# Three small reorderings in a one-core decoder layer: a low half behind a sum, two block loads dealt anew, and a stage's first loads one tile sooner

## The chip, the cores and the metric

The kernel runs on one core of a Trainium2 chip. The metric is the time of one execution on the device in microseconds (us), as the median of several runs. A profiled execution gives, besides its own time, a span: from the first to the last instruction on the core.

The engines are named as in the profile: PE is TensorE doing matmuls, PEld its weight loads (which overlap with the matmuls), DVE is VectorE, ACT is ScalarE, POOL is GpSimd, and SP (SPq) is the queue from which nearly all DMAs are issued. DMAs move data between the chip's main memory and the on-chip tiles; PSUM banks are where matmuls add up their results.

## The reference

One layer of a decoder over 1040 tokens (16 meta tokens and 1024 inputs), width 1024, float32. Cut to what matters here:

```python
a = rmsnorm(h, ln_mix_pre)
proj = a @ w_in                                    # 1024 x 3584
y_diff = diff_attention(...)                       # four heads, 512 wide
y_hgrn = hgrn2(...)                                # four heads, 512 wide
mix = concatenate([y_diff, y_hgrn], -1) @ w_out    # 1024 x 1024
h = h + rmsnorm(mix, ln_mix_post)
a = rmsnorm(h, ln_ffn_pre)
u = conv3(a @ w_up) + conv_b                       # 1024 x 5632, causal depthwise, width 3
gate, up = split(u, 2)
y = (gelu(gate) * up) @ w_down                     # 2816 x 1024
h = h + rmsnorm(y, ln_ffn_post)
return h[16:]                                      # meta tokens dropped
```

## The kernel before

**Precision.** Every float32 operand of a matmul is split into a high half (a cast to `fp32r` on ACT) and a low half (operand minus high half, on DVE or POOL): `split`, line 148. A product is then three matmuls: high by high, high by low, low by high. In the profile the halves of weights are `wh` and `wl` (`uh` and `ul` in the up stage), those of the down stage's left operand `gh` and `gl`, and those of the up stage's activations are both `t`.

**Order of the work.** PE runs in exactly the order of the program text. For every other engine and for the DMA queue a planner decides the order, from its own estimate of times and with the earlier text first where several things are ready; each engine then works its list strictly in that order. `tc.issue_after(x)` puts what is issued inside it behind `x` in the planned order. A tile (buffer) with a tag is reused by the next tile of that tag, and whoever writes it next waits until its last reader is done. So a change in the text moves both the planner's lists and the waits.

**Out-projection, second half of the columns** (loop at line 1281). Nine blocks of tokens, block 0 the meta tokens. For block `i` of 1 to 8, PE multiplies the block's mixed rows (1 MB with both halves, loaded from `msc` in two pieces by `second_load`, lines 1048 and 1055) with the weights `wo`. Three buffers hold blocks: "X1", "X2" and "mp". `SLOTS[1]` (line 1039) says which block uses which. At iteration `i` block `i + 1` is loaded and then the residual rows `xh` of block `i + 1` (`load_xh`, line 1190, two buffers). `post(i)` (line 1198) normalizes and adds the residual on ACT and DVE, stores the sum to `hsc`, and makes the normed rows `a2` (`a` in the profile); `trans(i - 2)` transposes an earlier block's normed rows on PE (line 1237) and ACT copies them to `at2` (`at`). After blocks 5 and 7 `t_split` splits finished quarters of `at2` for the up stage; the quarters 7 and 6 go into the buffers X2 and X1 that blocks have left.

**Up stage** (loop at line 1492, with `unit`, line 1372). The hidden width of 2816 is cut into 22 tiles `ft`; each tile has gate and up columns. The two halves of the contraction, of the tokens and gate against up make a 2 by 2 by 2 product that is done with seven products instead of eight (sums of weight quarters and of activation quarters are formed ahead). Tile 0 is done plainly. For the others, `unit(ft, p)` is one tile for token half `p`; both halves step in turn through products 0 to 6, each twelve matmuls (lines 1383 to 1385), into three PSUM banks: products 0 and 4 into `pa`, 1, 3 and 5 into `pb`, 2 and 6 into `pc`. Between them the partial results are read: ACT copies `x1` from `pa` after product 0, DVE forms u2 = pb + x1 after product 1, u3 = pb + x1 after product 3, and the outputs `uu` and `ug`. In the profile u2 and u3 are both `u`. Product 3 adds into the bank that u2 reads, so it must wait for u2, and likewise product 5 for u3. `gated` (line 1346) does the convolution (`c`), the gelu and the product, and stores to `gsc`. While tile `ft` is multiplied, `prep(7 * (ft + 1) + j)` (line 1139) prepares weight `j` of the next tile, at the head of step `j`: a sum of quarters on POOL (`w_sum`, for j of 0, 1, 3 and 6), the cast on ACT, the low half on POOL for j of 2, 4 and 6 and on DVE for j of 0, 1, 3 and 5.

**Down stage** (from line 1608). Seven products again, each over 11 pairs of tiles; `operands` loads and splits one pair, `LOOK` = 3 pairs ahead of PE (`ahead`, line 1530); the matmuls are at lines 1543 to 1545 (`pd`). The first three pairs are loaded (`opens`) and split inside the last tile of the up stage, at lines 1501 to 1506; with four buffers for `gi` and five for `wi`, the latter shared with the raw up weights.

Of the kernel before, what the change touches and what calls it, by code (L numbers as in the profile page):

```python
# [24 lines left out]
NF = DFF // P  # L25
HEADS = 4
NBLK = 9
# [58 lines left out]
def layer_kernel(ctx: ExitStack, tc: tile.TileContext, x, meta, table, lbl, gpre, gpost, win,  # L86
# [3 lines left out]
    V, A = Ordered(tc, nc.vector, state), Ordered(tc, nc.scalar, state)  # L90
    G = Ordered(tc, nc.gpsimd, state)
# [56 lines left out]
    def split(hi, lo, raw, eng=None, after=None):  # L148
        A.copy(hi, raw)
        with nullcontext() if after is None else tc.issue_after(after.ins):  # L150
            low = (eng or G).tensor_tensor(lo, raw, hi.bitcast(F32), op=ALU.subtract)
        if eng in (None, G):
            lows.append(low)
# [645 lines left out]
    raws, parts = {}, [[None, None] for _ in range(3)]  # L799
# [236 lines left out]
                yield from out_part(m0_7, py, wo[KD - 1:], range(1), False, False)  # L1036


    SLOTS = (("X1", "X2", "mp", "X1", "X2", "mp", "X1", "X2"), ("mp", "X1", "X2", "mp", "X1", "X2", "X1", "mp"))

    def block_tile(n, i):
        tag = SLOTS[n][i - 1]
# [12 lines left out]
    def second_load(i):  # L1055
        blocks[i] = block_tile(1, i)
        block_load(blocks[i], i, 0, 4)
        block_load(blocks[i], i, 4, 7 if i == 1 else 8)
# [63 lines left out]
    at2.reverse()  # L1122
    q_cm, qp = pool("p2", 2, "right")

    raws, sums, made = {}, {}, {}

    def load_raw4(ft):
        raws.clear()
# [10 lines left out]
    def prep(q):  # L1139
        ft, j = divmod(q, 7)  # L1140
        if ft >= NF or q in made:
            return
        if j == 0:
            load_raw4(ft)
            src = raws["11"]
            w_sum("1", raws["21"], raws["22"], ALU.add)
        elif j == 1:
            src = w_sum("2", sums["1"], raws["11"], ALU.subtract)
        elif j == 2:
            src = sums["1"]  # L1150
        elif j == 3:
            src = w_sum("3", raws["11"], raws["21"], ALU.subtract)
        elif j == 4:
            src = raws["12"]
        elif j == 5:
            src = raws["22"]
        else:
            src = w_sum("4", raws["12"], sums["2"], ALU.subtract)
        where = swp if q % 2 else wp
        hi = where.tile([P, 512], F32R, tag="wh", name=f"uh{q}", bufs=4)  # L1160
        lo = where.tile([P, 512], F32R, tag="wl", name=f"ul{q}", bufs=4)
        split(hi, lo, src, G if j % 2 == 0 and j else V)
        made[q] = (hi, lo)

    plain = {}
# [87 lines left out]
    def t_split(p, j, src, where, *tag):  # L1253
        hi, lo = t_tiles(p, j, where, tag)
        A.copy(hi, src)
        V.tensor_tensor(lo, src, hi.bitcast(F32), op=ALU.subtract)
        tt[p][j] = (hi, lo)

    def quarter(p, j):
        n = WN[p]  # L1260
        a, c = {0: (0, 0), 7: (0, n), 4: (4, 0), 6: (4, n)}[j]
        return at2[p][:, a:a + 4, c:c + n]
# [18 lines left out]
    for i in range(1, NBLK):  # L1281
        py = ps_b(f"py1_{i}")
        if i >= 3:
            y0_gain(i)
        if i == 1:
            load_xh(1)
            load_xh(0)
        if i + 1 < NBLK:
            second_load(i + 1)
            load_xh(i + 1)  # L1290
        run(blocks[i], py, wo, range(4), True, False)
        if i == 3:
            trans(1)
        run(blocks[i], py, wo, range(4, 7 if i == 1 else 8), False, i > 1)
        if i > 3:
            trans(i - 2)
        if i == 5:
            trans(0)
        if i == 1:
            pm = ps_b("py1_0")  # L1300
            for _ in meta_part(pm, wo, True):
                pass
            for p in range(3):
                out_last(p)
            run(k7(1), py, wo[KD - 1:], range(1), False, True)
            post(1, py)
            ysum = xhs.pop("sum")
            for l in range(2):
                A.copy(ysum[:2, 512 * l:512 * l + 512], pm[32 * l:32 * l + 2])
            G.tensor_tensor(ysum[:2, :512], ysum[:2, :512], ysum[:2, 512:], op=ALU.add)  # L1310
            for p in (3, 4):
                out_last(p)
            continue
        post(i, py)
        if i == 2:
            post(0, ysum[:, :512], ysum[:, 512:])
        if i == 5:
            t_split(0, 0, quarter(0, 0), ep, "e0")
            t_split(0, 4, quarter(0, 4), ep, "e1")
        if i == 7:  # L1320
            t_split(0, 7, quarter(0, 7), mxp, "X2", MIX["X2"])
            t_split(0, 6, quarter(0, 6), mxp, "X1", MIX["X1"])
        if i in (2, 3):
            for p in (1 + 2 * i, 2 + 2 * i):
                out_last(p)
# [2 lines left out]
    xu_cm, xup = pool("xu", 2)  # L1328
    t_cm, tp = pool("tsplit", 1)
    gap(tp, "gap1", 64)  # L1330

    marks = {}

    def outputs(ft, p):
        return [xup.tile([P, 2 * WN[0]], F32, tag=t, name=f"{t}{ft}_{p}") for t in ("ug", "uu")]
# [36 lines left out]
    def unit(ft, p, bank):  # L1372
        n = WN[p]
        nm = f"{ft}_{p}"
        ug, uu = outputs(ft, p)
        x1, u2, u3 = (xup.tile([P, WN[0]], F32, tag=t, name=f"{t}_{nm}")[:, :n] for t in ("x1", "u2", "u3"))

        def mm(j, pt, first):
            hi, lo = made[7 * ft + j]
            th, tl = tt[p][j]  # L1380
            for k in range(4):
                s = slice(P * k, P * (k + 1))
                T.matmul(pt, hi[:, s], th[:, k], start=(first and k == 0), stop=False, skip_group_check=True)  # L1383
                T.matmul(pt, hi[:, s], tl[:, k], start=False, stop=False, skip_group_check=True)  # L1384
                T.matmul(pt, lo[:, s], th[:, k], start=False, stop=(k == 3), skip_group_check=True)  # L1385

        pa = bank(f"pa{nm}")[:, :n]
        mm(0, pa, True)
        A.copy(x1, pa)
        yield  # L1390
        pb = bank(f"pb{nm}")[:, :n]
        mm(1, pb, True)
        marks[ft, p] = marks["last"] = V.tensor_tensor(u2, pb, x1, op=ALU.add)
        yield
        pc = bank(f"pc{nm}")[:, :n]
        mm(2, pc, True)
        yield
        mm(3, pb, False)
        V.tensor_tensor(u3, pb, x1, op=ALU.add)
        marks["last"] = V.tensor_tensor(uu[:, n:2 * n], pc, u3, op=ALU.add)  # L1400
        yield
        mm(4, pa, False)
        marks["left"] = A.copy(ug[:, :n], pa)
        yield
        mm(5, pb, False)
        marks["last"] = V.tensor_tensor(uu[:, :n], pb, x1, op=ALU.add)
        yield
        mm(6, pc, False)
        marks["last"] = V.tensor_tensor(ug[:, n:2 * n], pc, u2, op=ALU.add)
        gated(ft, p, ug, uu)  # L1410
        yield
# [25 lines left out]
    for j in range(4, 7):  # L1437
        prep(7 + j)
# [4 lines left out]
    keep, ready = {}, {}  # L1443
# [18 lines left out]
    def operands(pr, k, loaded=None):  # L1462
        ga, gb, gc, gs = (keep[nm][:, k] if keep else None for nm in ("ga", "gb", "gc", "gs"))
        if pr == 1:
            a = loaded[0] if loaded else g_in(k, 0, "1")
        elif pr == 2:
            SY.dma_start(gb, g_src(k + NH, 0))
            a = gb
        elif pr == 5:
            a = gs  # L1470
        elif pr == 6:
            V.tensor_tensor(gs, gs, ga, op=ALU.add)
            a = gs
        elif pr == 3:
            V.tensor_tensor(gb, gs, gb, op=ALU.subtract)
            a = gb
        elif pr == 7:
            V.tensor_tensor(ga, gc, ga, op=ALU.subtract)
            a = ga
        else:  # L1480
            a = g_in(k + NH, 1, "4")
        b = loaded[1] if loaded else w_in(pr, k)
        nm = f"{pr}_{k}"
        gh = dn.tile([P, 512], F32R, tag="gh", name=f"gh{nm}")
        gl = dn.tile([P, 512], F32R, tag="gl", name=f"gl{nm}")
        split(gh, gl, a, V)
        wh = wp.tile([P, 512], F32R, tag="wh", name=f"wh{nm}", bufs=4)
        wl = wp.tile([P, 512], F32R, tag="wl", name=f"wl{nm}", bufs=4)
        split(wh, wl, b, V)
        return gh, gl, wh, wl  # L1490

    for ft in range(1, NF):
        units = [unit(ft, p, ps_b) for p in range(2)]
        for j in range(7):
            prep(7 * (ft + 1) + j)
            for u in units:
                next(u)
            if (ft, j) == (1, 1):
                with tc.issue_after(marks[1, 1].ins):
                    next(p1)  # L1500
            if ft == NF - 1 and j == 1:
                with tc.issue_after(marks["store"].ins):
                    opens = [(g_in(k, 0, "1"), w_in(1, k)) for k in range(LOOK)]
            if ft == NF - 1 and j > 3:
                with tc.issue_after(marks["left"].ins):
                    ready[j - 4] = operands(1, j - 4, opens[j - 4])
    close(t2_cm, t_cm, xu_cm, mx_cm)

    f_cm, fp = pool("fin", 1)
# [185 lines left out]
```

## Time and profile before

| | us |
|---|---|
| median of three runs | 1302.69 (1301.43 to 1303.88) |
| the profiled execution | 1300.73 |
| its span | 1298.9 |

| engine | busy us | share of the span |
|---|---|---|
| PE | 1268.1 | 98% |
| PEld | 1179.0 | 91% |
| DVE | 887.0 | 68% |
| ACT | 695.1 | 54% |
| POOL | 482.6 | 37% |

Times in the profile are counted from the start of the span. In a timeline's row stand the start in us, the duration in us, the engine, the line of the kernel, the operation, the tile written and the tiles read (buffer numbers left out), the shapes, and, where the engine had been idle before, in square brackets how long and what ended it. Most operations of ACT, DVE and POOL go through one helper, so they all bear line 53 and are told apart by their tiles. Matmuls are pipelined: a row's duration is longer than the distance to the next start. The out-projection's second half lies at about 571 to 631, tile 0 of the up stage at about 631 to 656, the seven-product tiles from there to 1076, and the down stage from 1076 to the end.

### The profile page before, as it was taken

The numbers are of one execution on the slowest core, as the hardware profiler recorded it, in microseconds if no ns is written. First come the engines' busy times: TensorE is split into PE (matmuls) and PEld (weight loads), VectorE is DVE, ScalarE is ACT, GpSimd is POOL, SyncE is SP. The second block draws the span as 40 slices with busy tenths as digits, with TensorE's granted clock in tenths as the row PEclk, the third lists the DMA queues.
The fourth block names the chain that finished last, engine by engine and source line by source line (L and its number), as shares of the span: only waits on it lengthen the run. The fifth ranks groups of instructions, "written<-read, shape, count | busy, mean of one in ns | idle before, by whom it ended". The sixth has DMA issues, their size and how long they took to land.

```text
span 1298.9 us, 26100 instructions
## 1 busy us (share of the span) xinstructions
PE 1268.1 (98%) x10154; PEld 1179.0 (91%) x10154; DVE 887.0 (68%) x1488; ACT 695.1 (54%) x1639; POOL 482.6 (37%) x387
## 2 busy tenths in 40 slices
PE   8999999999999999999999999999999999999996
PEld 7999999899999998767899999999999998888885
DVE  7574646465645574547897877778778767697686
ACT  8465466546654764356854544544445435554553
POOL 5231423242323310353066575666665731010121
PEclk9999999999999999999999999999999999999999
DMA  6244655182644532787312222222222128964263
GB/s 215 94 99 89 120 120 116 47 156 78 125 116 86 122 103 90 222 272 265 117 67 82 90 75 82 74 89 83 74 75 90 66 79 274 336 203 170 90 211 122
DMA packets 116418, 165.04 MB, mean 127 GB/s; under 512 B 10099, under 2 KB 57523, under 8 KB 116294
## 3 DMA queue, kind: packets, MB, share of 16 engines
q1 hardware_dynamic: 93062, 151.84, 35.1%
q0 software_dynamic: 23232, 11.54, 7.6%
q8 instruction: 80, 1.31, 0.4%
q14 instruction: 44, 0.36, 0.1%
HBM read 134.24 MB, written 52.17 MB: 144 GB/s over the span
## 4 chain that ended last, share of the span: by engine, by line
PE 46%; DVE 4%; ACT 2%; issue 1%; DMA 1%; DVEq 0%; ACTq 0%
PE pd L1544 5%; PE pd L1545 5%; PE pd L1543 5%; PE pb L1383 5%; PE pb L1384 4%; PE pb L1385 4%; PE pa L1384 3%; PE pa L1383 3%; PE pa L1385 3%; PE pc L1384 3%; PE pc L1383 3%; PE pc L1385 3%; DVE c L53 1%; DVE t L53 1%; DVE xh L53 1%
## 5 line engine op out<-in xcount | busy, mean ns | idle before, releaser
L1383 PE MATMUL pb<-t,uh 128*128 128x258 f32 x504 | 142.5, 283 | 2.9 <-DVE u L53 2.7
L1384 PE MATMUL pb<-t,uh 128*128 128x258 f32 x504 | 141.2, 280 | 0.0
L1385 PE MATMUL pb<-t,ul 128*128 128x258 f32 x504 | 141.0, 280 | 0.0
L1544 PE MATMUL pd<-wl,gh 128*128 128x512 f32 x308 | 120.5, 391 | 2.0 <-DVE wl L53 2.0
L1545 PE MATMUL pd<-wh,gl 128*128 128x512 f32 x308 | 120.0, 390 | 0.0
L1543 PE MATMUL pd<-wh,gh 128*128 128x512 f32 x308 | 120.0, 390 | 0.0
L53 DVE SCALAR_TENSOR_TENSOR c<-uu,cwt,c 128x514 f32<-128x514 f32 (+1 forms) x88 | 96.5, 1096 | 19.6 <-ACT c L53 18.9
L53 POOL TENSOR_TENSOR c<-c,c 128x514 f32<-128x514 f32 (+1 forms) x44 | 63.8, 1449 | 122.3 <-ACT c L53 120.2
L1383 PEld LDWEIGHTS pb<-t,uh 128*128 128x128 f32 x504 | 95.0, 189 | 5.3 <-DVE u L53 5.3
L1385 PEld LDWEIGHTS pb<-t,ul 128*128 128x128 f32 x504 | 95.3, 189 | 0.0
L1384 PEld LDWEIGHTS pb<-t,uh 128*128 128x128 f32 x504 | 95.0, 188 | 0.0
L1384 PE MATMUL pa<-t,uh 128*128 128x258 f32 (+1 forms) x336 | 94.7, 282 | 0.0
L1383 PE MATMUL pa<-t,uh 128*128 128x258 f32 (+1 forms) x336 | 94.6, 281 | 0.0
L1385 PE MATMUL pa<-t,ul 128*128 128x258 f32 (+1 forms) x336 | 94.3, 281 | 0.0
L1384 PE MATMUL pc<-t,uh 128*128 128x258 f32 (+1 forms) x336 | 94.1, 280 | 0.0
L1385 PE MATMUL pc<-t,ul 128*128 128x258 f32 (+1 forms) x336 | 94.1, 280 | 0.0
L1383 PE MATMUL pc<-t,uh 128*128 128x258 f32 (+1 forms) x336 | 93.9, 279 | 0.0
L53 DVE SCALAR_TENSOR_TENSOR c<-ug,cwt,c 128x514 f32<-128x514 f32 (+1 forms) x88 | 88.3, 1004 | 1.4 <-ACT c L53 0.6
L53 ACT CAST uh<-ra 128x512 fp32r<-128x512 f32 x67 | 41.1, 617 | 63.2 <-PE pb L1384 42.0
L53 DVE TENSOR_TENSOR ul<-ra,uh 128x512 fp32r<-128x512 f32 x42 | 40.2, 957 | 48.7 <-ACT uh L53 48.7
L53 POOL TENSOR_TENSOR ul<-ws,uh 128x512 fp32r<-128x512 f32 x42 | 60.4, 1437 | 34.4 <-ACT uh L53 33.7
L1544 PEld LDWEIGHTS pd<-wl,gh 128*128 128x128 f32 x308 | 57.8, 188 | 15.5 <-DVE wl L53 3.7
(388 smaller groups left out, 4167.1 us busy)
## 6 DMA issues: line engine op xcount, KB each, us to landing
ra<-in_wup_dram SPq DMA_DIRECT2D x88, 256.0 KB, 2.6
mp<-msc SPq DMA_DIRECT2D x23, 512.0 KB, 5.0
tsc<-in_wdown_dram SPq DMA_DIRECT2D x44, 256.0 KB, 4.5
wi<-tsc SPq DMA_DIRECT2D x44, 256.0 KB, 2.7
gi<-gsc SPq DMA_DIRECT2D x33, 256.0 KB, 4.4
wi<-in_wdown_dram SPq DMA_DIRECT2D x33, 256.0 KB, 5.2
gsc<-c SPq DMA_DIRECT2D x22, 257.0 KB, 2.0
tsc<-in_wdown_dram POOLq DMA_DIRECT2D x22, 256.0 KB, 7.4
```

What stands on the lines that cost most here:

```text
L53: ins = call(*args, **kw)
L1383: T.matmul(pt, hi[:, s], th[:, k], start=(first and k == 0), stop=False, skip_group_check=True)
L1384: T.matmul(pt, hi[:, s], tl[:, k], start=False, stop=False, skip_group_check=True)
L1385: T.matmul(pt, lo[:, s], th[:, k], start=False, stop=(k == 3), skip_group_check=True)
L1543: T.matmul(py, gh[:, s], wh, start=(k == 0 and pr not in (3, 7)), stop=False, skip_group_check=True)
L1544: T.matmul(py, gh[:, s], wl, start=False, stop=False, skip_group_check=True)
L1545: T.matmul(py, gl[:, s], wh, start=False, stop=(k == NH - 1), skip_group_check=True)
```

## The change

It has three parts.

1. **Up stage.** In step `j = 1` the preparation of the next tile's weight 1 comes after both halves' product 1 in the text, no longer ahead of it, and its low half on DVE is put behind the u2 of token half 0 of the current tile (`marks[ft, 0]`). The dictionary `marks` is therefore made earlier in the text.
2. **Out-projection.** Of the last two blocks, 7 now uses "mp" and 8 uses X1, instead of the other way round. At iteration 5 blocks 6 and 7 are loaded, at iteration 6 block 8, at iteration 7 none; before, each iteration loaded the block after its own. The loads of `xh` keep their iterations. Because block 8 holds X1 to the end, the split of quarter 6 into X1 moves from after block 7 to after block 8.
3. **Down stage's start.** The first three pairs' loads move from step 1 of the last tile to step 5 of the tile before it, and so behind the stores of one tile earlier. Their splits move from steps 4, 5 and 6 of the last tile to steps 2, 3 and 4, and are put behind the last tile's `x1` copy and u2, instead of the `ug` copy after product 4 (`marks["left"]`).

```diff
-    SLOTS = (("X1", "X2", "mp", "X1", "X2", "mp", "X1", "X2"), ("mp", "X1", "X2", "mp", "X1", "X2", "X1", "mp"))
+    SLOTS = (("X1", "X2", "mp", "X1", "X2", "mp", "X1", "X2"), ("mp", "X1", "X2", "mp", "X1", "X2", "mp", "X1"))
...
-    raws, sums, made = {}, {}, {}
+    raws, sums, made, marks = {}, {}, {}, {}
...
-        split(hi, lo, src, G if j % 2 == 0 and j else V)
+        split(hi, lo, src, G if j % 2 == 0 and j else V, marks.get((ft - 1, 0)) if j == 1 else None)
...
         if i + 1 < NBLK:
-            second_load(i + 1)
+            for n in range(i + 1 if i < 6 else i + 2, min(i + 2 if i < 5 else i + 3, NBLK)):
+                second_load(n)
             load_xh(i + 1)
...
         if i == 7:
             t_split(0, 7, quarter(0, 7), mxp, "X2", MIX["X2"])
+        if i == 8:
             t_split(0, 6, quarter(0, 6), mxp, "X1", MIX["X1"])
...
-        A.copy(x1, pa)
+        marks["x1"] = A.copy(x1, pa)
...
         for j in range(7):
-            prep(7 * (ft + 1) + j)
+            if j != 1:
+                prep(7 * (ft + 1) + j)
             for u in units:
                 next(u)
+            if j == 1:
+                prep(7 * (ft + 1) + j)
             if (ft, j) == (1, 1):
                 with tc.issue_after(marks[1, 1].ins):
                     next(p1)
-            if ft == NF - 1 and j == 1:
+            if ft == NF - 2 and j == 5:
                 with tc.issue_after(marks["store"].ins):
                     opens = [(g_in(k, 0, "1"), w_in(1, k)) for k in range(LOOK)]
-            if ft == NF - 1 and j > 3:
-                with tc.issue_after(marks["left"].ins):
-                    ready[j - 4] = operands(1, j - 4, opens[j - 4])
+            if ft == NF - 1 and 1 < j < 5:
+                with tc.issue_after(marks["x1"].ins), tc.issue_after(marks[ft, 1].ins):
+                    ready[j - 2] = operands(1, j - 2, opens[j - 2])
```

More of the change, by code (lines that the diff above doesn't have):

```diff
@@ L1330, in layer_kernel @@
     gap(tp, "gap1", 64)
-    marks = {}
     def outputs(ft, p):
```

## The prediction

> **What bounds the kernel now.** I read the first page, then the busy time by stretches, then the waits of TensorE alone, and only then the timeline around each of those waits.
>
> ```profile
> span 1298.9 us, 26100 instructions
> PE 1268.1 (98%) x10154; PEld 1179.0 (91%) x10154; DVE 887.0 (68%) x1488; ACT 695.1 (54%) x1639; POOL 482.6 (37%) x387
> 690.00:730.00 40.00, 40.00 (x341) 39.81 (x340) 30.70 (x45) 19.09 (x34) 25.87 (x19) 1.00 0.24 82
> 639.70:673.30 33.60, 30.94 (x261) 30.54 (x259) 33.30 (x31) 24.81 (x39) 15.59 (x8) 1.00 0.11 40
> 1085.00:1127.00 42.00, 42.00 (x187) 34.77 (x186) 28.07 (x43) 20.74 (x35) 0.00 (x0) 1.00 1.02 361
> PE py L1020 <- DMA mp<-msc: 1.8, 1, 1.8
> PEld pb L1383 <- DVE u L53: 5.3, 12, 1.6
> PEld pd L1544 <- DVE wl L53: 3.7, 4, 1.8
> ```
>
> A row of stretches gives the stretch, its length, then busy time (and count) of PE, PEld, DVE, ACT and POOL, the granted clock, the DMA share and GB/s. A row of waits gives the total, how often, and the longest. TensorE is busy 98%, at clock 1.00 in all three stretches: the change removes no matmul, so it can only take away idle time on PE. The three waits are the three that it aims at: one DMA in the out-projection, twelve waits for VectorE in the up stage, and one of the four `wl` waits, at the start of the down stage. The second and third stretch matter for what is late next: in 639.7 to 673.3 it is DVE that is full (33.30 of 33.60), and in 1085 to 1127 the DMA engines are.
>
> **Up stage: the low half of product 1 behind u2.** The even tiles show it so (PE, then DVE):
>
> ```profile
> 687.44 0.28 PE L1385 MATMUL pc<-t,ul 128*128 128x256 f32 x1
> 687.75 0.39 PE L1383 MATMUL pb<-t,uh 128*128 128x258 f32 x1
> 687.98 0.28 PE L1384 MATMUL pb<-t,uh 128*128 128x258 f32 x1
> 684.31 2.45 DVE L53 SCALAR_TENSOR_TENSOR c<-ug,cwt,c 128x510 f32<-128x510 f32 x2
> 686.68 0.68 DVE L53 TENSOR_TENSOR ul<-ws,uh 128x512 fp32r<-128x512 f32 x1
> 687.29 0.74 DVE L53 TENSOR_TENSOR u<-pb,x 128x258 f32<-128x258 f32 x2
> 689.48 0.43 DVE L53 TENSOR_TENSOR u<-pb,x 128x258 f32<-128x258 f32 x1
> 693.55 0.28 PE L1383 MATMUL pb<-t,uh 128*128 128x258 f32 x1
> 707.62 0.28 PE L1383 MATMUL pb<-t,uh 128*128 128x258 f32 x1
> ```
>
> Product 3 of the first half adds into the bank that u2 reads, so it waits for u2. DVE comes late out of the convolution (684.31), does the next tile's low half (686.68) and only then u2. Starts on PE are otherwise 0.12 apart (341 in the 40 us above); here 0.31 and then 0.23, so 0.19 + 0.11 = 0.30 us are lost. With u2 ahead, it ends 0.60 sooner (the distance 686.68 to 687.29), about 687.05, half a microsecond before PE asks for it at 687.56. The odd tiles (707.62) do not wait. Of the twelve waits ten are of this kind: 10 x 0.30 = 3.0 us, and I count all of it. What the low half then pushes is u3 (689.48), which has until 693.55. The cast on ACT and the sum on POOL move by one step in the text as well; both are for the next tile and cost nothing unless their queues are full (ACT 19 and POOL 26 of 40 us).
>
> The other two waits are in the first tile of the seven-product loop, and there I count nothing:
>
> ```profile
> 665.98 0.39 PE L1383 MATMUL pb<-t,uh 128*128 128x258 f32 x1 [1.28 <-DVE u L53]
> 672.89 0.41 DVE L53 TENSOR_TENSOR u<-pb,x 128x258 f32<-128x258 f32 x1
> 673.36 0.39 PE L1383 MATMUL pb<-t,uh 128*128 128x258 f32 x1 [1.45 <-DVE u L53]
> ```
>
> The first wait gets 0.60 shorter, but the second is the end of a DVE backlog that has run almost without a gap since 639.7: the same work, the moved pass too, stands ahead of the u3 at 672.89, so the second wait grows by what the first loses. Bounds: 0 if the order stays so, 0.60 to the good if the low half slips behind that u3 too, as much to the bad if one more gets ahead. I take 0.
>
> **Out-projection: blocks 7 and 8 change buffers and are asked for one block sooner.** SP, PE and DVE:
>
> ```profile
> mp<-msc SPq DMA_DIRECT2D x14, 512.0 KB, 7.9
> 604.49 0.53 SPq L1048 DMA_DIRECT2D mp<-msc x1
> 607.02 0.40 PE L1024 MATMUL py<-woh,mp 128*128 128x512 f32 x1
> 608.70 0.53 SPq L1048 DMA_DIRECT2D mp<-msc x1
> 610.66 1.82 SPq L1048 DMA_DIRECT2D mp<-msc x2
> 615.54 1.03 PE L1237 MATMUL pa<-ident,a 128*128 128x128 f32 x8
> 617.02 0.33 SPq L1196 DMA_DIRECT2D xh<-in_x_dram x1
> 618.36 0.47 PE L1020 MATMUL py<-woh,mp 128*128 128x512 f32 x1 [1.78 <-DMA mp<-msc]
> 624.70 1.28 DVE L53 SCALAR_TENSOR_TENSOR a<-xh,ssy,gfb 128x1024 f32<-128x1024 f32 x1 [1.78 <-ACT ssy L53]
> 633.00 1.28 DVE L53 SCALAR_TENSOR_TENSOR a<-xh,ssy,gfb 128x1024 f32<-128x1024 f32 x1
> 634.33 0.86 PEld L1237 LDWEIGHTS pa<-ident,a 128*128 128x128 f32 x8 [0.32 <-DVE a L53]
> ```
>
> The first of these rows is of the issues from 570 to 640: halves of 512 KB, 7.9 us to landing at the median. Block 5 frees X1 with the matmul at 607.02. The half issued at 604.49 therefore isn't X1's: it and the one at 608.70 are block 8's, into "mp", and block 7, which waits for X1, goes out last, at 610.66. PE wants it about 616.3 (after eight transposes from 615.54, 0.1 apart) and gets it at 618.36: 2.0 us. After the change block 7 has the places at 604.49 and 608.70: by 7.9 us it lands at 612.4 and, its second half, at 616.6, which PE wants at 619. Block 8 has the place at 610.66 and is wanted at about 622.6. The wait goes. On SP the loads of x for blocks 6 and 7 now stand behind block 7's and block 8's halves; both buffers come free (by 607.02) ahead of the x load at 617.02, so that costs nothing. But what is late next is the transpose of block 7's normed rows: PE already waits there (634.33) for the DVE result of 633.00, whose chain hangs on the loads of x, issued at 617.02 and later, behind the row stores in the same DMA rush; the change moves no x load ahead. PE would come 2.0 us sooner and wait there 2.0 longer. Nor would time saved there help before DVE's backlog ends at 672.89. X1's split waits for block 8's matmuls now instead of block 7's, a cast and a 1.2 us DVE pass that must be done by about 638. So the net: from -1.2 (that pass comes in DVE's way once) to +2.0 (DVE starts its backlog that much sooner, since a full block load less stands ahead of the x loads). I take 0.
>
> **Down stage: first loads and casts sooner.**
>
> ```profile
> 1069.73 0.38 ACT L53 COPY ug<-pa 128x258 f32<-128x258 f32 x1 [6.26 <-PE pa L1385]
> 1081.96 0.39 PE L1543 MATMUL pd<-wh,gh 128*128 128x512 f32 x1
> 1082.96 0.68 DVE L53 TENSOR_TENSOR wl<-wi,wh 128x512 fp32r<-128x512 f32 x1
> 1083.69 0.50 PE L1544 MATMUL pd<-wl,gh 128*128 128x512 f32 x1 [1.34 <-DVE wl L53]
> 1084.03 0.40 PE L1545 MATMUL pd<-wh,gl 128*128 128x512 f32 x1
> 1084.80 0.33 SPq L1351 DMA_DIRECT2D gsc<-c x1
> 1090.55 0.62 ACT L53 CAST gh<-gi 128x512 fp32r<-128x512 f32 x1 [3.34 <-DMA gi<-gsc]
> ```
>
> The third operand's low half (1082.96) stands on DVE behind the last convolution. Starts are 0.23 apart here; 1.73 and 0.34 lose 1.50 + 0.11 = 1.6 us. With the casts allowed after the last tile's u2, ACT does them in its 6.26 us of idle time before 1069.73, and DVE, which is as free then, follows. Then the fourth operand has DVE from about 1082.4, 1.3 us of work, and is wanted at 1084.7. The loads that are moved, six of 256 KB, go out nearly a tile earlier, when the DMA engines are little used (share 0.24). On SP they pass the two stores of the last tile but one, which now stand behind them; the weight loads wait for raw weight tiles that the last preparation frees at that very step, and nobody reads those stores before the down stage: no cost. The price is later: the fifth or sixth operand's load stands on SP behind the last store (1084.80) and lands at 1090.55, in a stretch in which DMA is full. PE that runs 1.6 us sooner needs it sooner; but the freed buffers also let one or two loads pass ahead of that store. Bounds 0 to 1.6 gained; I take 1.6, by the row of the idle time.
>
> **Sum.** 3.0 + 0 + 0 + 1.6 = 4.6 us. The profiled execution took 1300.73 (span 1298.9), 1.96 below the median of 1302.69, so it becomes about 1296.1, and the median **1298.1**.
>
> **The rivals.**
> *More: the out-projection keeps its gain.* The same sum with up to 2.0 us more: 1296.1. For it: DVE has gaps there (1.78 us ahead of 624.70) that earlier data could fill. Against it: what ends that gap hangs on an x load, which isn't moved.
> *Less: one of the two sources dries up.* The down stage's 1.6 lost in the DMA rush leaves 3.0, 1299.7; the even tiles' waits staying, because the planner puts another DVE pass before u2, leaves 1.6, 1301.1.
> *Nothing: the planner orders every queue but PE's itself*, and could leave them as they are: 1302.7.
> *Slower: the low half stands in front of u3.* In every one of 20 tiles, odd ones too, it takes a place just behind u2, when POOL is at work. A low half costs there more than the 0.68 above:
>
> ```profile
> 713.99 1.63 DVE L53 TENSOR_TENSOR ul<-ra,uh 128x512 fp32r<-128x512 f32 x1 [2.46 <-ACT uh L53]
> 713.79 1.29 POOL L53 TENSOR_TENSOR ul<-ra,uh 128x512 fp32r<-128x512 f32 x1
> ```
>
> It decides where u3 ends past 693.55, that is 3.6 us late; two such passes and a wait for a cast would be needed. A wait of one low half, 0.60, in each tile costs 20 x 0.60 = 12.0: 1302.69 - 4.6 + 12.0 = 1310.1. [...]
>
> **How the numbers follow.** Forecast 0.47, more 0.16, less 0.17, nothing 0.06, slower 0.14. 0.2% is 2.6 us, about what runs of this kernel can tell from no change. Forecast and "more" are beyond it; "less" is half beyond it (3.0) and half not (1.6): faster 0.72, same 0.08 + 0.06 = 0.14, slower 0.14. The range goes from the end of "more", 1296.1, to that of "less", 1301.1, with 0.6 at either side for a median of three runs that spread over 2.5: 1295.5 to 1301.7. It leaves out "nothing" and "slower".
>
> **What would show it.** Right: the group of PEld waits for `u` falls from 12 to two, those of the first tile, with tiles 19.7 apart throughout; the wait for `mp` is gone, and a wait of about 2 us for `a` stands in its place; no wait of `pd` for `wl` near the start of the down stage. Wrong: PE waits of 0.2 us or more for `u` in the odd tiles, a new wait of `pd` for a load, or the product 5 of the first tile starting later than now against the start of the out-projection.

## The result and the profile after

The changed kernel takes 1298.72 us (median of 7 runs, 1296.03 to 1299.89) against 1302.69 (7 runs, 1300.73 to 1303.88): 4.0 us less, ratio 0.997 [0.9961, 0.998]. The forecast was 1298.1 in 1295.5 to 1301.7. The profiled executions took 1296.03 and 1300.73, 4.7 us apart, where the sum said 4.6.

The page and the waits of the changed kernel:

```profile
span 1294.2 us, 26076 instructions
PE 1265.5 (98%) x10154; PEld 1178.6 (91%) x10154; DVE 884.7 (68%) x1488; ACT 694.4 (54%) x1639; POOL 486.9 (38%) x387
690.00:730.00 40.00, 40.00 (x343) 40.00 (x342) 30.12 (x45) 19.55 (x35) 27.54 (x20) 1.00 0.25 81
656.00:676.00 20.00, 16.24 (x136) 15.83 (x135) 19.56 (x22) 9.86 (x17) 17.82 (x10) 1.00 0.24 80
PEld pb L1383 <- DVE u L53: 4.2, 2, 2.7
PEld pa L1237 <- DVE a L53: 2.8, 3, 1.7
PEld pd L1547 <- DVE wl L53: 2.1, 3, 0.8
```

The steady tiles have no idle weight load left (40.00 of 40.00). Twelve waits for `u` are two, but these two cost 4.2 us where the twelve cost 5.3. The fourth wait for `wl` is gone; the wait for `mp` is not among the waits any more, and one more wait for `a` is there.

Where the time went is read best from the start of the same matmul in both traces. Both do the same matmuls up to the out-projection, and still stand up to 0.8 us apart within that part, so differences are counted from the matmul that stands at 590.34 before. The stretches end at the matmuls that stand at 690.69, 1045.40 and 1289.00 (the last) before. The later experiments are split in the same way, against the same trace of before (us; minus is sooner). Stretches that an edit leaves alone still differ by 0.1 to 0.9 from one trace to the next, most of all in the last column.

| Kernel | out-projection and first tile, to 691 | steady tiles, to 1045 | last tiles and down stage | together |
|---|---|---|---|---|
| whole change | -0.5 | -2.7 | -1.6 | -4.7 |
| part 1 alone (up stage) | -0.4 | -2.7 | -0.1 | -3.2 |
| part 2 alone (out-projection) | +1.3 | -0.1 | +0.5 | +1.7 |
| part 3 alone (down stage) | +0.2 | +0.2 | -1.5 | -1.1 |
| parts 1 and 3 | +1.1 | -2.7 | -1.8 | -3.3 |
| whole change, low half three times | +2.2 | +1.6 | -0.4 | +3.4 |
| whole change, three low halves on POOL | +3.7 | -2.7 | -0.9 | +0.1 |
| whole change, convolution later | +1.5 | -2.7 | -0.7 | -1.8 |
| parts 1 and 3, convolution later | +2.1 | -2.7 | -1.3 | -1.9 |
| part 2, convolution later | +3.6 | +0.2 | +0.8 | +4.6 |
| part 2, 24 matmuls more | +0.2 | +0.1 | -0.2 | +0.1 |

### The profile page after: what moved, and what is told of

Read it like the earlier page. It is cut to its first block, busy times and chain, and to the rows that moved or that the text cites. A ratio compares the mean times of both kernels' runs of the same rounds, so it can differ in the third digit from the quotient of the medians.

```text
span 1294.2 us, 26076 instructions
## 1 busy us (share of the span) xinstructions
PE 1265.5 (98%) x10154; PEld 1178.6 (91%) x10154; DVE 884.7 (68%) x1488; ACT 694.4 (54%) x1639; POOL 486.9 (38%) x387
## 4 chain that ended last, share of the span: by engine, by line
PE 47%; DVE 4%; ACT 2%; issue 1%; DMA 1%; DVEq 0%; SPq 0%; ACTq 0%
PE pd L1547 5%; PE pd L1548 5%; PE pd L1546 5%; PE pb L1383 4%; PE pb L1384 4%; PE pb L1385 4%; PE pa L1384 3%; PE pa L1383 3%; PE pc L1384 3%; PE pa L1385 3%; PE pc L1383 3%; PE pc L1385 3%; DVE c L53 1%; DVE xh L53 1%; DVE wl L53 1%
```

## The experiments

**The parts by themselves.** The first takes from the diff only what concerns the low half of product 1: the later call of `prep` in the tile loop, and the marker that holds it behind u2.

> Part 1 alone (next tile's low half of weight 1 behind u2). Theory (each part takes away its own wait, and the parts add): the ten even-tile waits go, 10 x 0.31 = 3.1 us between the end of the first seven-product tile and the down stage; the two waits of the first tile stay about 3 us together; sum -3.1 us, about 1299.6. Rival (DVE order is one queue, so part 1 needs the others' slack): the waits stay or move to the odd tiles, 0 us.

1299.72 against 1302.09, ratio 0.9981 [0.9971, 0.9991]. The waits for `u` of its trace:

```profile
PEld pb L1381 <- DVE u L53: 3.5, 2, 2.6
```

Two are left, those of the first tile. The first of them has shrunk from 1.47 to 0.86, the second has grown from 1.65 to 2.62, and from the first product 5 of the first tile to the end of the up stage 3.0 us are gained, as the whole change gains there.

The second experiment has only the new SLOTS, the earlier second_load and the low half of (0, 6) one block later.

> Part 2 alone (blocks 7 and 8 dealt anew). Theory (the DVE backlog to 673 sets when the up stage runs on): PE starts block 7 about 2 us sooner or more, and at product 5 of the first seven-product tile no more than 0.4 us are left of it; sum -0.4 to 0, so no difference that the runs can tell. Rival (time won on PE ahead is kept): -2 us, 1300.7.

1304.11, ratio 1.0018 [1.0008, 1.0027]: slower than the kernel before, by 2.0, which no side expected. Its trace, TensorE behind the last wait of the first tile, then the stretch's busy times and clock, then VectorE ahead of it:

```profile
675.40 0.39 PE L1385 MATMUL pb<-t,uh 128*128 128x258 f32 x1 [3.90 <-DVE u L53]
...
676.43 0.42 PE L1385 MATMUL pb<-t,uh 128*128 128x258 f32 x1
676.64 0.42 PE L1386 MATMUL pb<-t,uh 128*128 128x258 f32 x1
676.00:680.00 4.00, 4.00 (x23) 4.00 (x22) 3.00 (x5) 0.81 (x1) 3.07 (x3) 0.58 0.18 67
673.26 1.75 DVE L53 TENSOR_TENSOR ul<-ws,uh 128x512 fp32r<-128x512 f32 x1
674.93 0.41 DVE L53 TENSOR_TENSOR u<-pb,x 128x258 f32<-128x258 f32 x1
```

TensorE did come sooner out of the out-projection: it starts product 4 of the first tile (668.90 before) 2.3 us sooner, counted from 590. VectorE does not: u3 ends its backlog at 674.93, 0.1 later than before by the same count; the low half in front of it takes 1.75 (0.68 before). So all that was gained turns into idle time, 3.90 instead of 1.45. And shortly behind it the matmuls come 0.21 apart instead of 0.12, for 3.4 us (676.0 to 679.4; the granted clock is 0.58 over the 4 us shown): 1.5 us lost that the kernel before does not lose.

The third experiment has only the loads and casts of the down stage.

> Part 3 alone (down stage's first loads and casts sooner). Theory: the wait of pd for wl at the third operand goes, -1.6 us, and all of it is kept through the stretch in which DMA is full; about 1301.0. Rival (the DMA rush takes it back): a new wait of pd within ten operands, 0 to -0.5 us.

1300.12, ratio 0.9988 [0.9979, 0.9996], 2.0 less. The wait for `wl` at the start of the down stage is gone, and 1.5 us with it:

```profile
PEld pd L1544 <- DVE wl L53: 2.0, 3, 0.8
```

The fourth has the first and the third part without the second.

> Parts 1 and 3 without part 2. Theory (sums add, part 2 is worth nothing): -4.7 us, about 1298.0, the same as the whole change. Rival (part 2 carries a piece of the gain): 1 us or more slower than the whole change.

1297.96, ratio 0.9975 [0.9963, 0.9987]: the same as the whole change within the intervals. Its profiled execution shows that the slow stretch is not part 2's own:

```profile
673.38 0.58 PE L1381 MATMUL pb<-t,uh 128*128 128x258 f32 x1 [2.37 <-DVE u L53]
673.76 0.42 PE L1382 MATMUL pb<-t,uh 128*128 128x258 f32 x1
673.00:676.00 3.00, 2.62 (x12) 2.62 (x13) 2.84 (x5) 0.96 (x3) 3.00 (x3) 0.56 0.23 87
```

Half clock follows a wait of 2.37 here, where behind 2.51 in the whole change's trace and 2.42 in part 1's the clock stayed at 1.00.

**Two edits that make a part work or not.** The fifth changes the place of prep in the text as part 1 does, without the marker.

> Part 1 with the text moved but without the order to stand behind u2 (the low half of weight 1 is prepared after both halves' product 1 in the text, and the planner may put it where it likes). Theory (the planner thinks DVE is free before u2 is ready and fills the gap with the low half, so only the explicit order helps): the ten waits of 0.2 us for u stay; 0 us in the steady tiles. Rival (the text's order is enough): the ten waits go, -3.1 us.

1301.65, one run, beside 1302.12. Its waits for `u`:

```profile
PEld pb L1383 <- DVE u L53: 5.8, 12, 2.6
```

All twelve stay: the planner puts the low half back ahead of u2 (686.50 and 687.10 in this trace), whatever the order of the text. The marker does the work of part 1. The sixth has part 3's earlier loads without the earlier casts.

> Of part 3 only the loads sooner; the casts stay in steps 4 to 6 of the last tile behind the ug copy. Theory (the third operand is late because its low half stands behind the last convolution on DVE, not for want of data): the wait of pd for wl of 1.3 us stays, 0 us. Rival (the data came late): the wait goes, -1.6 us.

1301.67, one run; the four waits for `wl`, 3.7 us, stay as they were:

```profile
PEld pd L1544 <- DVE wl L53: 3.7, 4, 1.8
```

The earlier loads alone bring nothing; part 3 needs the earlier casts. Earlier casts without earlier loads were not run.

**How much room is behind u2?** The seventh does the moved low half three times.

```diff
         split(hi, lo, src, G if j % 2 == 0 and j else V, marks.get((ft - 1, 0)) if j == 1 else None)
+        if j == 1 and (ft - 1, 0) in marks:
+            for _ in range(2):
+                with tc.issue_after(marks[ft - 1, 0].ins):
+                    V.tensor_tensor(lo, src, hi.bitcast(F32), op=ALU.subtract)
```

> The whole change, with the moved low half done three times in each of the tiles: two DVE passes more, 0.7 to 1.6 us each, between u2 and u3 (the result is the same). Theory (there are 3.6 us between u3 and product 5): u3 comes 1.4 to 3.2 us later and PE still does not wait for it; steady tiles stay 19.7 us apart, 0 to +1 us against the whole change, at most from the first tile's backlog. Rival (the moved low half has used up DVE's slack): a wait of 0.6 us or more in each of 20 tiles, +12 us.

1306.44, ratio 1.004 [1.0027, 1.0053], 8 us above the whole change. VectorE and TensorE in a steady tile:

```profile
710.86 2.37 DVE L53 TENSOR_TENSOR ul<-ws,uh 128x512 fp32r<-128x512 f32 x2
713.16 0.41 DVE L53 TENSOR_TENSOR u<-pb,x 128x256 f32<-128x256 f32 x1
713.49 3.14 DVE L53 TENSOR_TENSOR ul<-ws,uh 128x512 fp32r<-128x512 f32 x2
716.55 0.41 DVE L53 TENSOR_TENSOR u<-pb,x 128x258 f32<-128x258 f32 x1
713.40 0.28 PE L1389 MATMUL pb<-t,ul 128*128 128x258 f32 x1
713.62 0.39 PE L1387 MATMUL pb<-t,uh 128*128 128x256 f32 x1
713.85 0.28 PE L1388 MATMUL pb<-t,uh 128*128 128x256 f32 x1
```

Two low halves get in front of u2 of the second half (713.16), and TensorE loses 0.10 + 0.11 = 0.21 at 713.62. Against the whole change that is 4.2 us over 18 tiles, 0.24 each. u3 is not late: with two more passes it still ends in time. A further 2.7 lie in the first tile, where the wait for u3 is 3.66 and half clock follows it (0.61 in 676 to 680).

**Can POOL take over some of VectorE's backlog?** The eighth is the whole change with the low halves of three activation sums on POOL, which is idle there until about 650 (for 46.26 us up to 652.82 in the whole change's trace).

```diff
+    ON_POOL = ((0, 2), (0, 3), (0, 5))
...
-        V.tensor_tensor(lo, src, hi.bitcast(F32), op=ALU.subtract)
+        (G if (p, j) in ON_POOL else V).tensor_tensor(lo, src, hi.bitcast(F32), op=ALU.subtract)
```

> The whole change, and three low halves of activation sums (products 2, 3 and 5 of token half 0, 128x1032 each) made on POOL instead of DVE, where POOL is idle from about 606 to 655. Theory (DVE's backlog sets when product 5 of the first seven-product tile can start): 3 x 1.14 = 3.4 us less on DVE ahead of u3, the two waits of the first tile shrink by 2 to 3.4 us in all, about 1295.8. Rival A (POOL's passes lock DVE out, or POOL is late with a low half that product 2 or 3 needs): gain under 1 us or a loss. Rival B (PE is held in the first tile by something else than DVE's backlog): no change.

1302.41, ratio 0.9999 [0.999, 1.0008], 3.7 above the whole change. POOL, VectorE and TensorE:

```profile
644.93 8.95 POOL L53 TENSOR_TENSOR t<-at,t 128x1032 fp32r<-128x1032 f32 x3 [36.59 <-ACT t L53]
648.57 6.39 DVE L53 TENSOR_TENSOR t<-at,t 128x1024 fp32r<-128x1024 f32 x2
655.02 0.39 PE L1366 MATMUL pq<-t,uh 128*128 128x256 f32 x1 [1.50 <-DVE t L53]
670.88 0.39 PE L1384 MATMUL pb<-t,uh 128*128 128x258 f32 x1 [3.16 <-DVE u L53]
671.44:674.86 3.42, 3.42 (x18) 3.42 (x17) 3.42 (x5) 2.15 (x5) 2.27 (x2) 0.50 0.02 5
```

Three passes cost POOL 3 us each, and two of VectorE's own beside them 3.2 each instead of the 1.2 that they take alone: what was taken off VectorE it loses in these longer passes, and `t` comes late. So does u2, by 3.16 us for TensorE, and half clock follows that wait too.

**What sits between the out-projection and the steady tiles?** Three kernels put the convolution of the zeroth tile's second half behind u3 of the first tile's second half, instead of behind u2: its four passes stood on VectorE just ahead of the u3 that TensorE waits for.

```diff
-        V.tensor_tensor(u3, pb, x1, op=ALU.add)
+        third = V.tensor_tensor(u3, pb, x1, op=ALU.add)
+        if (ft, p) == (1, 1):
+            with tc.issue_after(third.ins):
+                next(p1)
...
-            if (ft, j) == (1, 1):
-                with tc.issue_after(marks[1, 1].ins):
-                    next(p1)
```

> The whole change, and the convolution of the zeroth tile's second half behind u3 of the first tile's second half on VectorE instead of behind u2. Nothing is left out. Theory: the last wait for u of the first tile (2.51 us in the changed kernel's trace, u3 at 672.64 though its bank was complete at about 664.8) is made of those four convolution passes ahead of u3; with them behind it the wait is gone, product 5 starts at about 670.6, and the time falls by 2.2 to 2.5, to about 1296.4. A granted clock under 1.00 right behind that wait cannot occur any more either. Rival, the backlog only moves: the same passes are then late for the sums uu of the second half or for u2 of the next tile, TensorE waits there for what it no longer waits for at u3, and the time stays at 1298 to 1299, with a new PEld wait of 1.5 us or more between 673 and 690.

1300.68, ratio 0.9988 [0.9977, 0.9999]: 2 us above the whole change, more than either side expected. Its long wait in the up stage:

```profile
691.01 0.39 PE L1383 MATMUL pb<-t,uh 128*128 128x258 f32 x1 [2.41 <-DVE u L53]
```

It is for u2 of the second tile, as the rival said, and its clock stays at 1.00. The same edit on parts 1 and 3:

> Parts 1 and 3 without part 2, with the same move of the convolution. Nothing is left out. Theory: the wait of 2.37 us goes and with it the stretch of 3.4 us behind it in which the matmuls stood 0.21 apart instead of 0.12 (granted clock 0.56), which cost 1.1 in that trace and not in every execution: 1297.96 less 2.4 less up to 1.1, about 1295. Part 2 then makes a difference of 0.3 or less between this run and the one with the whole change, since the wait for u2 at 666 still takes up what part 2 brings ahead of it. Rival, part 2 keeps its gain once the last wait is gone: this run is 1.5 to 2 us slower than the one with the whole change. Rival, the backlog only moves: 1297 to 1298.

1298.59, ratio 0.9979 [0.997, 0.9988], not faster than without it. Its waits between the first and the second tile, and the clock behind the last:

```profile
675.40 0.19 PEld L1381 LDWEIGHTS pc<-t,uh 128*128 128x128 f32 x1 [0.75 <-DVE uu L53]
687.95 0.19 PEld L1381 LDWEIGHTS pb<-t,uh 128*128 128x128 f32 x1 [2.64 <-DVE u L53]
684.00:690.00 6.00, 3.56 (x24) 3.36 (x23) 5.54 (x8) 3.07 (x6) 3.34 (x3) 0.85 0.28 80
```

The wait for u3 is gone, and the same time is lost at the next two sums, 0.75 for uu and 2.64 for u2 of the second tile, with half clock behind it again. The same edit on part 2 alone:

> Part 2 alone, with the same move of the convolution. Nothing is left out. Part 2 alone was 2 us slower than the kernel before, and its trace shows why by the theory: TensorE reaches the last wait of the first tile 2.3 us sooner, u3 comes no sooner, the wait grows to 3.90, and the matmuls behind it run 3.4 us at a granted clock of 0.58, 1.5 us lost that the kernel before doesn't lose. Theory: without the wait both go, 1304.1 less 3.9 less 1.3, about 1299, 3 faster than the kernel before. Rival, the slow clock has nothing to do with the wait: the stretch at 0.21 apart stays, and the time is 1300.2 or more. Rival, part 2 is slower for another reason (loads of x late, contention): 1301.5 to 1302.

1304.86, ratio 1.0026 [1.0017, 1.0035]; the theory said 1299 and fails. The waits stand where those of the run before stand, 1.62 for uu on TensorE and then 2.75 for u2 of the second tile. That wait, the clock behind it, and two earlier stretches:

```profile
692.64 0.39 PE L1385 MATMUL pb<-t,uh 128*128 128x258 f32 x1 [2.75 <-DVE u L53]
691.62:695.03 3.41, 2.39 (x20) 2.39 (x21) 2.78 (x7) 1.66 (x3) 2.64 (x2) 1.00 0.65 207
633.59:637.00 3.41, 1.33 (x12) 1.12 (x12) 2.46 (x3) 3.32 (x11) 0.00 (x0) 1.00 0.35 142
637.00:640.42 3.42, 3.42 (x19) 3.42 (x17) 3.38 (x5) 2.40 (x5) 0.00 (x0) 0.50 0.16 63
```

Behind these 2.75 us of waiting the clock stays at 1.00. But the trace has a stretch at half clock elsewhere, from 637.0 to 640.4, behind a wait of 2.08 for `a` at the end of the out-projection; the matmuls that stand at 634.6 to 656.0 before take 1.1 us longer here than in part 2's trace. So this execution has a slow stretch all the same, as the others seem to (mean granted clock over the executions 0.9964, part 2 alone 0.9962), and the run can't tell whether an idle time causes it.

By the count from 590 this run begins the steady tiles 3.6 us later than the kernel before. What the new order costs in all three kernels stands in VectorE's busy time between the matmuls that stand at 590.34 and 690.69 before (us):

| Kernel | VectorE busy without the new order | with it | matmul at 690.69 later by |
|---|---|---|---|
| whole change | 89.36 | 91.20 | 2.0 |
| parts 1 and 3 | 90.80 | 91.68 | 1.0 |
| part 2 | 90.13 | 92.41 | 2.3 |

VectorE has as many passes as without it, within one, but they take longer, and the steady tiles begin later by about as much. Which passes these are, and why they are longer, was not sorted out. So the new order moved the waits, and added to VectorE's work.

**Is it the idle time that slows the clock?** The last kernel is part 2 alone with product 4 of the first tile's second half done three times, 24 matmuls in the middle of the long wait. The order on VectorE, ScalarE, POOL and SP is that of part 2.

```diff
-        mm(4, pa, False)
+        for _ in range(3 if (ft, p) == (1, 1) else 1):
+            mm(4, pa, False)
```

> Part 2 alone, and product 4 of the first tile's second half added three times instead of once: 24 matmuls more, 2.8 us of TensorE work, inside the wait of 3.90 us for u3; that tile's gate half is then not the reference's. Nothing moves on the other engines. Theory: the stretch of 3.4 us at half clock behind that wait (matmuls 0.21 apart, granted clock 0.58, 1.5 us lost) comes of the idle time itself, so with the wait cut to about 1.1 the clock stays at 1.00, product 5 starts where it did, and the kernel gets faster by the added work: part 2's 1304.1 less 1.5, about 1302.6, and the mean granted clock of the executions goes from 0.9962 to about 0.9975. Rival, the slow stretch has another cause (the load on the array or on the chip at that point): it stays, 1304.1. Rival, TensorE sets the end here: 2.8 more, 1306.9.

```profile
673.17 0.39 PE L1385 MATMUL pb<-t,uh 128*128 128x258 f32 x1 [1.09 <-DVE u L53]
...
674.00 0.28 PE L1385 MATMUL pb<-t,uh 128*128 128x258 f32 x1
674.11 0.28 PE L1386 MATMUL pb<-t,uh 128*128 128x258 f32 x1
673.00:676.00 3.00, 2.83 (x23) 2.83 (x24) 2.93 (x6) 0.00 (x0) 3.00 (x3) 1.00 0.23 90
```

1302.64, ratio 1.0007 [0.9998, 1.0016]. The matmuls behind the wait come 0.12 apart at clock 1.00, and the table of stretches shows part 2's +1.3 fall to +0.2: with 2.8 us of work added, this stretch is 1.2 us shorter. The intervals of the two ratios overlap a little, so the medians alone do not prove it; the mean granted clock over the executions speaks more clearly: 0.9976 here (11 runs; 0.9975 for the kernel before beside it, 15 runs), 0.9962 for part 2 alone (12 runs; 0.9976 for the kernel before beside it, 32 runs). (It is not 1.00 for the kernel before: its trace is at half clock in its last microseconds, from 1294.67 on, behind the last matmul, as the whole change's is from 1289.25 on.) One stretch of 3.4 us at half clock takes 3.4 x 0.5 / 1300 = 0.0013 off that mean, so part 2 alone has about one more of them in each execution and this kernel none. The whole change has 0.9973 (7 runs) and parts 1 and 3 have 0.9971 (9 runs): by the same working, an estimate, it is there one execution in four to one in three.

## Why the prediction was right, and where it was not

**Up stage, 3.0: right, in size and mechanism.** VectorE in a steady tile of the changed kernel:

```profile
686.47 0.41 DVE L53 TENSOR_TENSOR u<-pb,x 128x258 f32<-128x258 f32 x1
686.81 0.68 DVE L53 TENSOR_TENSOR ul<-ws,uh 128x512 fp32r<-128x512 f32 x1
687.41 0.41 DVE L53 TENSOR_TENSOR u<-pb,x 128x256 f32<-128x256 f32 x1
```

u2 stands ahead of the low half, as foreseen. From product 5 of the first tile (673.36 to 673.11) to 1045.40 (now 1042.18) 3.22 - 0.25 = 2.97 us are gained, and two tiles take 39.4. The marker, not the text, makes it so. The rival with the low half in front of u3 did not come about: in the steady tiles the moved low half takes 0.68 in every one, not the 1.63 that the prediction set against it, and even three low halves do not make u3 late. What they bring is a place in front of u2 of the second half, at 0.24 a tile instead of the 0.60 by which I priced it.

**First tile's two waits, 0: right.** Product 5 behind them starts only 0.2 to 0.3 sooner than before. In part 1 alone the first wait lost the 0.60 that was foreseen (1.47 to 0.86) and the second gained 0.97; in the whole change, where part 2 brings TensorE to them sooner still, the first stays (1.47 to 1.46) and the second grows by 1.06. The rows of the whole change:

```profile
633.05 0.86 PEld L1237 LDWEIGHTS pa<-ident,a 128*128 128x128 f32 x8 [1.72 <-DVE a L53]
666.10 0.19 PEld L1383 LDWEIGHTS pb<-t,uh 128*128 128x128 f32 x1 [1.46 <-DVE u L53]
673.10 0.19 PEld L1383 LDWEIGHTS pb<-t,uh 128*128 128x128 f32 x1 [2.71 <-DVE u L53]
665.97 1.43 DVE L53 TENSOR_TENSOR ul<-ws,uh 128x512 fp32r<-128x512 f32 x1
672.64 0.74 DVE L53 TENSOR_TENSOR u<-pb,x 128x258 f32<-128x258 f32 x2
```

In this first tile the moved low half takes 1.43 at 665.97, with POOL at work for 0.88 of it, where before it took 0.68 ahead of u2 (at 664.91): nearer to the 1.63 that the rival of the slower side set against 0.68. u3 comes at 672.64, 0.25 sooner than before, against 0.06 sooner at 590.

**Out-projection, 0 net: right for the whole change, with the right reason, and incomplete for part 2 itself.** Block 7 starts 2.7 us sooner (618.36 to 615.68), the wait of 1.72 for `a` at 633.05 takes 1.4 of that, and VectorE's backlog takes the rest, as the step said. SP shows block 7's two loads in their new places:

```profile
603.84 0.53 SPq L1048 DMA_DIRECT2D mp<-msc  x1
608.05 0.53 SPq L1048 DMA_DIRECT2D mp<-msc  x1
```

What the step lacked is that TensorE's idle time cost more behind it: after the 3.90 in part 2's trace the matmuls stood 0.21 apart instead of 0.12 for 3.4 us. By itself part 2 costs 2.0, outside the bounds that I gave it (1.2 lost to 2.0 gained), and of the 1.7 in its trace the half clock has 1.5; no row of the trace before shows it, since the waits at that place were 1.28 and 1.45. In the whole change the same price is paid in some executions (by the mean clocks, an estimate), so part 2 adds nothing that these runs can tell: parts 1 and 3 without it measure 0.9975 against 0.997.

**Down stage, 1.6: right.** The casts go to the idle time on ScalarE (the first at 1057.64, 1071.41 before), and one of the waits for `wl` that stay takes back a little, 0.62 where it was 0.46:

```profile
1057.64 0.62 ACT L53 CAST gh<-gi 128x512 fp32r<-128x512 f32 x1
1144.47 0.19 PEld L1547 LDWEIGHTS pd<-wl,gh 128*128 128x128 f32 x1 [0.62 <-DVE wl L53]
```

From 1045.40 to the fourth pair of down-stage operands the gain grows by 1.8, and 0.2 is given back by the end, 1.58 in all. The load behind the last store did not become a wait of TensorE.

**The sum** was 4.6; the profiled executions differ by 4.7, the medians by 4.0. That the medians gain less is not settled. The half clock that one execution in four to one in three has would make it about 0.4, an estimate, and the spread of seven runs (3.9) leaves room for the rest.

## What to carry to other kernels

A wait is worth removing where nothing late stands behind it: three reorderings took away 3.0, 1.6 and 2.0 us of waiting, and only the first two arrived at the end, because behind the third VectorE was full until 673 (33.30 of the 33.60 us from 639.7 in the trace before). So ask first which engine's total work sets the next meeting point; if it is another engine's, coming sooner only means waiting longer. Six waits of 2.08 to 3.90 us cost TensorE a second time here, 1.1 to 1.6 us behind them, and the one into which 24 matmuls were put no longer did. And check in the planned order that a move in the text moves anything at all: for part 1 only the marker did.

## What the runs showed of the hardware

Behind some of its waits TensorE lost time twice. After waits of 2.08, 2.37, 2.44, 3.16, 3.66 and 3.90 us the matmuls stood 0.21 apart instead of 0.12 for 3.4 us (granted clock 0.50), a price of 1.1 to 1.6; after 1.45, 2.41, 2.42, 2.51 and 2.75 us elsewhere they did not. 24 matmuls put into the wait of 3.90 left 1.09 of it, and the clock behind it at 1.00. So the length of a wait alone does not decide it. The 3.4 us that end where the half clock begins, in the traces of part 2 and of parts 1 and 3:

```profile
672.56:675.98 3.42, 0.58 (x4) 0.58 (x5) 3.39 (x5) 1.34 (x4) 3.34 (x3) 1.00 0.00 0
669.95:673.36 3.41, 1.05 (x9) 0.85 (x8) 3.38 (x6) 1.60 (x4) 2.05 (x2) 1.00 0.00 0
```

TensorE was busy for 0.58 and 1.05 us in them, still at clock 1.00. In the whole change's trace it was busy for 0.90 of the 3.41 us ahead of product 5 (669.70 to 673.11), and the clock stayed at 1.00 behind them (673.11 to 677). What else decides it, no experiment here was made to find. By the mean clocks (0.9962 and 0.9973), part 2 alone pays in about every execution and the whole change in some, an estimate.

Side by side, VectorE and POOL did not slow each other evenly. While VectorE went through passes of 1.2 us almost without a gap, one of POOL's low halves (128x512) took 7.24 us in the whole change's trace and 4.95 in the one before, where later ones take 1.3 to 1.8. In the eighth experiment three of POOL's passes took 3.0 each, and two of VectorE's beside them 3.2 each instead of 1.2; a low half of 512 columns took VectorE 0.68 to 0.69 where POOL was idle, and beside it 0.69 (at 656.46 in the whole change's trace, beside the 7.24), 1.43 (at 665.97) and up to 1.77 (in the eighth experiment).

```profile
652.82 7.24 POOL L53 TENSOR_TENSOR ul<-ra,uh 128x512 fp32r<-128x512 f32 x1 [46.26 <-ACT uh L53]
```
